# Hybrid decoder trunk on one core: five unread matmuls after the index products, and a separate gate table for the first two expert pairs

## The chip, the core and the metric

The kernel runs on one core of a Trainium2 chip, as one launch that holds the whole network. The metric is the time of one execution in microseconds (us); lower is better. The kernel before takes 1132.8 us in the median of three runs (1131.58 to 1132.91 us).

## What is computed

One decoder layer over 512 tokens of width 1024 in float32: a mixer of two branches, cross-attention into 256 memory tokens, and a mixture of 32 experts. The change lies where the mixture begins:

```python
g_idx = argmax(g_logits); p_g = softmax(g_logits)[g_idx]        # one of 4 groups
e_in_group = take_along_axis(e_logits, g_idx)                   # 8 experts in it
top_v, top_i = lax.top_k(e_in_group, 2)
gate = p_g * softmax(top_v)                                     # two gates per token
# every expert's tokens, in blocks:
xb = xt[tok]; hb = silu(xb @ w1[e]) * (xb @ w3[e]); out = hb @ w2[e]
y[token] += gate * out
```

`xt` is the RMS-normed stream. The kernel gathers rows of the stream that are not normed yet and lets the norm factor of a token (`rr`) travel with its gates.

## The kernel before, in words

The whole program is written out in Python in the order in which each engine is to work; each engine runs its own instructions in that order. TensorE is `PE`, VectorE `DV` (DVE in the profile), ScalarE `AC`, GpSimd `PO` (POOL). Weights arrive by DMAs that SyncE (SP) issues.

**The experts.** An expert's token block holds up to 64 rows (`CAP`); two blocks make a pair and share one gather. For a block, `up` (line 1245) multiplies the gathered rows by w1 and w3: 16 products of 64x512 in full float32, each of which shows as two matmul records, so 32 records; the first 16 use the first halves of w1 and w3, the other 16 the second halves. Then come `act` (silu and product, lines 1256 and 1257), `turn_h` (transposes, lines 1264 and 1267) and `down` (w2, line 1275).

**The weights.** An expert has six tiles of 1 MB (`half_load`, line 733). They go into 19 buffers of that size (`NSLOT`). By the end of the attention part 19 tiles have been asked for; the next two loads are asked for behind the first half of the first `up` (`moe_load(2)` at `k % 4 == 3`), since they need the buffers that this half reads, and so on: every later load waits for a buffer that some product has finished with. SP issues them in order.

**The start of the mixture**, which the change touches:

- The last routing logits are made (line 957), and DVE picks the group and the two experts per token. Meanwhile `warm(..., 4)` (lines 97 to 103) gives TensorE four products of 128x512 whose result nobody reads (`wu`).
- `pp` (line 1037) counts, by 14 small products, the place of each token in its expert's block; `posm` (line 1043) holds the places.
- `tbl` is a table with, for every token, its number (two columns, written early by GpSimd at line 921), the high and low part of its norm factor `rr` (lines 1057 and 1058), and the high and low parts of its gates.
- For the first two pairs, `onehots` (line 1189) makes a matrix that marks which token sits in which place, and `from_tokens` (line 1196) multiplies it with the two number columns of `tbl`: that is the index product. DVE turns its result into an index (line 1201), and GpSimd issues the gather (line 1203).
- `gating` computes the gates (DVE, lines 1063 to 1083) and writes those of the first four experts into `tbl` by `gate_parts` (lines 1054 and 1055).
- `gather_turn` transposes the gathered rows (PE, line 1229) and scales them into `xg` (DVE, line 1185), and `up_of(0)` multiplies them: the first `up`.
- The two gate products (line 1196 again, now 8 columns of `tbl`), `places` (the rest of the routing, DVE, lines 1090 to 1142), and `gates_of` (lines 1215 and 1216), which feeds `act` of the first block, follow.

Of the kernel before, what the change touches and what calls it, by code (L numbers as in the profile page):

```python
# [25 lines left out]
F32 = mybir.dt.float32  # L26
F32R = mybir.dt.float32r
# [3 lines left out]
OP = mybir.AluOpType  # L31
AX = mybir.AxisListType

P = 128
D = 1024
S = 512
T = S // P
# [12 lines left out]
NBLK = NE + 2  # L50
DYN = 4
# [3 lines left out]
def trunk(ctx: ExitStack, tc: tile.TileContext, a: dict, out: bass.AP, dbg=None):  # L55
    nc = tc.nc
    PE, DV, AC, PO = nc.tensor, nc.vector, nc.scalar, nc.gpsimd

    cst = ctx.enter_context(tc.tile_pool(name="cst", bufs=1))
# [25 lines left out]
    def k2(shape, dt=F32, name="k2"):  # L85
        return view(big, shape, dt, name, "k2", 7, (S + 3) * (2 if dt == BF else 1))

    def sm(shape, dt=F32, name="sm"):
        return view(big, shape, dt, name, "sm", 22, 16)

    def md(shape, dt=F32, name="md"):
        return view(big, shape, dt, name, "md", 5, T * NBLK * (2 if dt == BF else 1))

    def bank(shape, dt=F32, name="ps"):
        return view(psp, shape, dt, name, "ps", 8, 512)

    def warm(a_, b_, n, ps=None):

        if ps is None:
            ps = bank([P, 512], name="wu")  # L100
        for _ in range(n):
            PE.matmul(ps, a_, b_, start=True, stop=True)
# [6 lines left out]
    x_sb = cst.tile([P, T, D], F32, name="x_sb")  # L109
# [17 lines left out]
    ident = cst.tile([P, P], F32, name="ident")  # L127
# [784 lines left out]
    rr = cst.tile([P, T], F32, name="rr")  # L912
# [3 lines left out]
    tbl = cst.tile([P, T, 1 + NB, 4], F32R, name="tbl")  # L916
    tk0 = md([P, T, 2], name="tk0")
# [2 lines left out]
            allow_small_or_imprecise_dtypes=True)  # L920
    PO.tensor_copy(tbl[:, :, 0, 0:2], tk0)

    def cols(t, p):
        return tbl[:, t, 0:2 + p:1 + p]

# [73 lines left out]
    def b2(ap, shape):  # L999
        return ap.to_broadcast(shape)  # L1000
# [23 lines left out]
    def spread(dst, src):  # L1024
        DV.tensor_tensor(dst.rearrange("p t (g e) -> p t g e", g=4),
                         goh[:, :, :, None].to_broadcast([P, T, 4, 8]),
                         src[:, :, None, :].to_broadcast([P, T, 4, 8]), op=OP.mult)
# [18 lines left out]
    perm = cst.tile([P, NBLK], F32, name="perm")  # L1046
    permi = cst.tile([P, NBLK], I32, name="permi")

    def gate_parts(b0, b1, src):

        for t in range(T):
            hi, lo = (tbl[:, t, 1 + b0 // 2:1 + b1 // 2, q:4:2] for q in range(2))
            g_ = src[:, t].rearrange("p (n e) -> p n e", e=2)
            DV.tensor_copy(hi, g_)
            DV.tensor_tensor(lo, g_, hi.bitcast(F32), op=OP.subtract)

    DV.tensor_copy(tbl[:, :, 0, 2], rr)
    DV.tensor_tensor(tbl[:, :, 0, 3], rr, tbl[:, :, 0, 2].bitcast(F32), op=OP.subtract)

    def gating():  # L1060

        ge = md([P, T, 4], name="gexp")
        DV.tensor_tensor(ge, gl, b2(gm, [P, T, 4]), op=OP.subtract)
        AC.activation(ge, ge, AF.Exp)
        gs = sm([P, T, 1], name="gsum")
        DV.tensor_reduce(gs, ge, axis=AX.X, op=OP.add)
        dd = sm([P, T, 1], name="dd")
        DV.tensor_sub(dd, m2, m1)
        AC.activation(dd, dd, AF.Exp)
        den = sm([P, T, 1], name="den")  # L1070
        DV.scalar_tensor_tensor(den, dd, 1.0, gs, op0=OP.add, op1=OP.mult)
        g1 = sm([P, T, 1], name="g1")
        DV.reciprocal(g1, den)
        g2 = sm([P, T, 1], name="g2")
        DV.tensor_mul(g2, g1, dd)
        gt8 = md([P, T, 8], name="gt8")
        DV.tensor_tensor(gt8, oh1, b2(g1, [P, T, 8]), op=OP.mult)
        gt8b = md([P, T, 8], name="gt8b")
        DV.tensor_tensor(gt8b, oh2, b2(g2, [P, T, 8]), op=OP.mult)
        DV.tensor_add(gt8, gt8, gt8b)  # L1080
        gate = md([P, T, NE], name="gate")
        spread(gate, gt8)
        DV.tensor_tensor(gate, gate, b2(rr[:, :, None], [P, T, NE]), op=OP.mult)
        gate_parts(0, DYN, gate[:, :, 0:DYN])
        return gate

    def places(gate):

        cnt = md([P, NE], name="cntf")
        DV.tensor_copy(cnt, pp[:, T])  # L1090
        ov = md([P, NE], name="ov")
        DV.scalar_tensor_tensor(ov, cnt, float(CAP), wgt, op0=OP.is_gt, op1=OP.mult)
        DV.tensor_tensor(ov, ov, isp, op=OP.max)
        om = sm([P, 1], name="om")
        DV.tensor_reduce(om, ov, axis=AX.X, op=OP.max)
        DV.tensor_scalar(ov, ov, om, None, op0=OP.is_equal)
        nv = md([P, NE], name="nv")
        DV.tensor_scalar(nv, ov, -1.0, 1.0, op0=OP.mult, op1=OP.add)
        R = 2 * T + 2
        yy = k2([P, R, NE], name="yy")  # L1100
        DV.tensor_tensor(yy[:, 0:T], pp[:, 0:T], off_, op=OP.add)
        DV.tensor_copy(yy[:, T:2 * T], gate)
        DV.tensor_copy(yy[:, 2 * T], cnt)
        DV.tensor_copy(yy[:, 2 * T + 1], io32)
        zz = k2([P, R, NE], name="zz")
        yv = sm([P, R, 1], name="yv")
        DV.tensor_tensor(zz, yy, b2(ov[:, None, :], [P, R, NE]), op=OP.mult)
        DV.tensor_reduce(yv, zz, axis=AX.X, op=OP.add)
        DV.tensor_tensor(zz, b2(yy[:, :, POS:POS + 1], [P, R, NE]), b2(ov[:, None, :], [P, R, NE]), op=OP.mult)
        DV.tensor_tensor(yy, yy, b2(nv[:, None, :], [P, R, NE]), op=OP.mult)  # L1110
        DV.tensor_tensor(yy, yy, zz, op=OP.add)
        DV.tensor_copy(yy[:, :, POS:POS + 1], yv)

        def spaced(dst, src, second, c0=0):

            DV.tensor_copy(dst[:, :, c0:POS + 1], src[:, :, c0:POS + 1])
            DV.tensor_copy(dst[:, :, POS + 2:NBLK - 1], src[:, :, POS + 1:NE])
            DV.tensor_scalar(dst[:, :, POS + 1:POS + 2], src[:, :, POS:POS + 1], second, None, op0=OP.add)

        cn = md([P, 2, NBLK], name="cn")  # L1120
        DV.memset(cn, 0.0)
        spaced(cn[:, 1:2], yy[:, 2 * T + 1:2 * T + 2], 0.0)
        DV.tensor_copy(perm, cn[:, 1])
        DV.tensor_copy(permi, cn[:, 1])
        spaced(posm, yy[:, 0:T], -float(CAP), DYN)
        DV.memset(posm[:, :, NBLK - 1:NBLK], -4096.0)
        gb = md([P, T, NBLK], name="gb")
        DV.memset(gb[:, :, NBLK - 1:NBLK], 0.0)
        spaced(gb, yy[:, T:2 * T], 0.0)
        gate_parts(DYN, NBLK, gb[:, :, DYN:NBLK])  # L1130
        spaced(cn[:, 0:1], yy[:, 2 * T:2 * T + 1], -float(CAP))
        c_ = cn[:, 0]
        DV.memset(c_[:, POS:POS + 1], 0.0)
        nx = k2([P, NBLK, 7], name="nx")
        DV.tensor_tensor(nx, c_[:, :, None].to_broadcast([P, NBLK, 7]),
                         io7[:, None, :].to_broadcast([P, NBLK, 7]), op=OP.is_gt)
        nxr = md([P, NBLK], name="nxr")
        DV.tensor_reduce(nxr, nx, axis=AX.X, op=OP.add)
        one = md([P, NBLK], name="one")
        DV.memset(one, 1.0)  # L1140
        DV.tensor_tensor_scan(cume, one, nxr, 0.0, op0=OP.mult, op1=OP.add)
        DV.tensor_copy(total, cume[:, NBLK - 1:NBLK])
# [44 lines left out]
    def onehots(p):  # L1187
        oh = k2([P, T, 2, CAP], F32R, name="oh")
        DV.tensor_tensor(oh, io64[:, None, None, :].to_broadcast([P, T, 2, CAP]),
                         posm[:, :, 2 * p:2 * p + 2, None].to_broadcast([P, T, 2, CAP]), op=OP.is_equal)  # L1190
        return oh

    def from_tokens(pg, oh, rhs, start=True):

        for t in range(T):
            PE.matmul(pg, oh[:, t].rearrange("p n c -> p (n c)"), rhs(t), start=t == 0, stop=t == T - 1)
# [9 lines left out]
    def tokens_of(pg):  # L1206
        tk = sm([P, 1], name="tk")
        DV.tensor_scalar(tk, pg[:, 0:1], float(S), None, op0=OP.add)
        return tk
# [149 lines left out]
    pgs, gcs, tks, xrs, xgs, ohs, ups = {}, {}, {}, {}, {}, {}, {}  # L1359
# [13 lines left out]
    for p in range(2):  # L1373
        oh = ohs[p] = onehots(p)
        pgs[p] = bank([P, 8], name="pgate")
        from_tokens(pgs[p][:, 0:2], oh, lambda t: tbl[:, t, 0, 0:2])
        xrs[p] = gather_two(pgs[p])
        tks[p] = tokens_of(pgs[p])
    gate = gating()
    xgs[0] = gather_turn(xrs.pop(0))  # L1380
    up_of(0)
    for p in range(2):
        pgs[p] = bank([P, 8], name="pgate")
        from_tokens(pgs[p], ohs.pop(p), lambda t: cols(t, p))
    places(gate)
    for p in range(2):
        gcs[p] = gates_of(pgs[p])
# [5 lines left out]
    for b in range(LASTB + 1):  # L1393
        p, par = divmod(b, 2)
# [23 lines left out]
        if b == LASTB - 2:  # L1418
            left()
            g_f = slot([P, D], name="g_f")  # L1420
            src = a["norm_f_g"]
# [77 lines left out]
```

## Time and profile before

| | |
|---|---|
| median of 3 runs | 1132.8 us (1131.58 to 1132.91) |
| the profiled execution's own time | 1134.74 us |
| its span, first to last instruction | 1132.9 us |
| PE busy | 1092.2 us (96%) |
| DVE busy | 571.9 us (50%) |
| ACT busy | 370.4 us (33%) |
| POOL busy | 117.3 us (10%) |
| granted TensorE clock, mean over the span | 0.988 of full |
| read from HBM | 272.88 MB |

The profile shows one execution. The span is counted from its first instruction to its last; the execution's own time, taken around it, is 1.84 us longer, and it is 1.94 us above the median of the three runs. PE counts as busy while a matmul record is open, so a busy PE need not work at its peak: it also stands so at half clock. The page's slices give the granted clock (PEclk), which here is full nearly throughout and dips around the start of the mixture, and the share of the DMA engines that was busy.

### The profile page before, as it was taken

What the parts mean: (1) busy time and instruction counts of PE and PEld (TensorE: products, weight loads), DVE (VectorE), ACT (ScalarE), POOL (GpSimd) and SP (SyncE); (2) the same over time, 40 slices, a digit from 0 to 9 for tenths busy, and PEclk for the clock granted to TensorE, in tenths of its full rate; (3) what the DMA queues carried; (4) which work ended last, traced back from release to release, by engine and by line L of the source; (5) the groups of instructions that cost most, each with busy time, mean ns of one, the idle gap of its engine ahead of it and who ended that gap; (6) DMA issues with size and microseconds to landing.
All of it is one profiled execution on the core that took longest, in us unless ns stands there. A gap on an engine that the chain in (4) does not pass through costs nothing. (4 is left out here: it accounts for less than half of the span.)

```text
span 1132.9 us, 14115 instructions
## 1 busy us (share of the span) xinstructions
PE 1092.2 (96%) x5297; PEld 725.5 (64%) x5297; DVE 571.9 (50%) x1116; ACT 370.4 (33%) x634; POOL 117.3 (10%) x157
## 2 busy tenths in 40 slices
PE   5999999999999999999999899999999999999995
PEld 4778888888888888898888634444444444443432
DVE  5376574655434566673563464444444444443444
ACT  4366644554442533553443111111111111111112
POOL 4021000200120200000200100000010000000001
PEclk9999999999999999999999889999999999999998
DMA  9122141214323163233249669999999999999981
GB/s 323 51 75 75 53 159 60 75 47 149 112 82 113 38 246 119 88 138 126 81 155 384 240 276 424 426 426 425 426 426 426 425 427 426 425 426 427 426 349 74
DMA packets 62501, 273.29 MB, mean 241 GB/s; under 512 B 6976, under 2 KB 7104, under 8 KB 37856
## 3 DMA queue, kind: packets, MB, share of 16 engines
q1 hardware_dynamic: 57616, 260.15, 57.3%
q0 software_dynamic: 4096, 9.61, 2.4%
q10 hardware_dynamic: 720, 2.62, 0.6%
q8 instruction: 42, 0.69, 0.2%
q14 instruction: 27, 0.22, 0.1%
HBM read 272.88 MB, written 4.19 MB: 245 GB/s over the span
## 5 line engine op out<-in xcount | busy, mean ns | idle before, releaser
L1245 PE MATMUL h<-we,xg 128*64 128x512 f32 x1056 | 240.2, 597 | 6.7 <-DMA we<-in_w 6.1
L1245 PEld LDWEIGHTS h<-we,xg 128*64 128x64 f32 x1056 | 78.4, 138 | 162.0 <-issue 142.5
L276 PE MATMUL acc<-whi,xh 128*128 128x512 f32 x448 | 177.5, 396 | 0.0
L278 PE MATMUL acc<-wlo,xh 128*128 128x512 f32 x448 | 175.3, 391 | 0.7 <-POOL v L379 0.7
L277 PE MATMUL acc<-whi,xl 128*128 128x512 f32 x448 | 175.3, 391 | 0.0
L168 DVE TENSOR_TENSOR wlo<-raw,whi 128x1024 fp32r<-128x1024 f32 x101 | 119.9, 1232 | 47.8 <-ACT whi L167 43.7
L1275 PE MATMUL po<-we,hT 128*64 128x512 f32 x528 | 120.6, 599 | 1.7 <-ACT hT L1267 1.7
L167 ACT CAST whi<-raw 128x1024 fp32r<-128x1024 f32 x104 | 102.9, 1048 | 8.5 <-PE acc L278 4.9
L1282 ACT CAST o_h<-po 64x512 fp32r<-64x512 f32 x66 | 38.2, 579 | 187.9 <-PE po L1275 187.1
L278 PEld LDWEIGHTS acc<-wlo,xh 128*128 128x128 f32 x448 | 84.3, 188 | 19.2 <-POOL v L379 1.1
L277 PEld LDWEIGHTS acc<-whi,xl 128*128 128x128 f32 x448 | 84.5, 189 | 16.5 <-DVE xl L254 0.4
L276 PEld LDWEIGHTS acc<-whi,xh 128*128 128x128 f32 x448 | 84.5, 189 | 16.2 <-ACT xh L253 0.2
L1283 DVE TENSOR_TENSOR o_l<-po,o_h 64x512 fp32r<-64x512 f32 x66 | 45.4, 688 | 74.3 <-ACT o_h L1282 73.2
L1275 PEld LDWEIGHTS po<-we,hT 128*64 128x64 f32 x528 | 35.0, 136 | 65.0 <-issue 53.7
L317 PE MATMUL acc<-xh,whi 128*128 128x512 f32 x192 | 75.3, 392 | 0.4 <-ACT whi L167 0.4
L319 PE MATMUL acc<-xh,wlo 128*128 128x512 f32 x192 | 74.9, 390 | 0.8 <-DVE wlo L168 0.8
L318 PE MATMUL acc<-xl,whi 128*128 128x512 f32 x192 | 74.8, 390 | 0.0
L1267 ACT COPY hT<-phT 128x256 f32<-128x256 f32 x33 | 12.3, 372 | 187.0 <-PE phT L1264 186.9
L1293 DVE TENSOR_TENSOR x_sb<-x_sb,pc 128x512 f32<-128x512 f32 x120 | 72.9, 679 | 0.0
L1185 DVE TENSOR_TENSOR xg<-pgT,g_moe 128x512 f32<-128x512 f32 x34 | 21.9, 686 | 96.6 <-PE pgT L1229 96.6
L1291 PE MATMUL pc<-o_h,ohT 128*128 128x512 f32 x120 | 48.4, 404 | 0.0
L1292 PE MATMUL pc<-o_l,ohT 128*128 128x512 f32 x120 | 47.3, 395 | 0.0
(340 smaller groups left out, 1492.1 us busy)
## 6 DMA issues: line engine op xcount, KB each, us to landing
we<-in_w SPq DMA_DIRECT2D x192, 1024.0 KB, 20.1
raw<-in_w_in SPq DMA_DIRECT2D x31, 1024.0 KB, 5.0
raw<-in_w_xkv SPq DMA_DIRECT2D x8, 1024.0 KB, 4.9
raw<-in_w_out SPq DMA_DIRECT2D x4, 1024.0 KB, 6.4
raw<-in_w_xq SPq DMA_DIRECT2D x4, 1024.0 KB, 6.2
raw<-in_w_xo SPq DMA_DIRECT2D x4, 1024.0 KB, 5.3
x_sb<-in_x SPq DMA_DIRECT2D x4, 512.0 KB, 5.6
xn_d<-x_sb ACTq DMA_DIRECT2D x4, 512.0 KB, 2.9
```

The lines of the kernel that those rows point to most:

```text
L167: AC.copy(hi[:, s], raw[:, s])
L168: (PO if i + q == 1 or (i, q) == (4, 1) else DV).tensor_tensor(lo[:, s], raw[:, s], hi[:, s].bitcast(F32), op=OP.subtract)
L276: PE.matmul(ps, lh, rh, start=first, stop=False)
L277: PE.matmul(ps, ll, rh, start=False, stop=False)
L278: PE.matmul(ps, lh, rl, start=False, stop=last)
L317: PE.matmul(ps[m], hi[:, k, ms], xh, start=first, stop=False)
L318: PE.matmul(ps[m], hi[:, k, ms], xl, start=False, stop=False)
L319: PE.matmul(ps[m], lo[:, k, ms], xh, start=False, stop=last)
L1245: PE.matmul(ps[i * 64:(i + 1) * 64], xg[:, k, xs_], w[n, k // 4][:, k % 4], start=k == 0, stop=k == 7)
L1275: PE.matmul(po[dh][dh * 64:(dh + 1) * 64], hT[:, f], w["2", f // 2][:, f % 2, dh * 512:(dh + 1) * 512], start=f == 0, stop=f == 3)
L1291: PE.matmul(ps, oT_[r, t], o_h[dh][r], start=True, stop=False)
L1293: DV.tensor_add(x_sb[:, t, cs], x_sb[:, t, cs], ps)
```

## The change

There is a second, small table `tb0`, which holds for every token the two number columns, the norm factor's two parts and the gates of the first four experts. GpSimd fills its number columns early, beside those of `tbl`. The index products and the gate products of the first two pairs read `tb0` in place of `tbl`. The two DVE instructions that write the norm factor's parts move from ahead of the index products into `gating`, and write `tb0`. Once `places` has written the gates of the other experts into `tbl`, two DVE copies bring `tb0`'s norm factor and gates over to `tbl`, which the later pairs read as before. And behind the second index product TensorE gets five more unread products of 128x512.

```diff
+    tb0 = cst.tile([P, T, 3, 4], F32R, name="tb0")
+    PO.tensor_copy(tb0[:, :, 0, 0:2], tk0)
...
-    def gate_parts(b0, b1, src):
+    def gate_parts(b0, b1, src, tbl):
...
-    DV.tensor_copy(tbl[:, :, 0, 2], rr)
-    DV.tensor_tensor(tbl[:, :, 0, 3], rr, tbl[:, :, 0, 2].bitcast(F32), op=OP.subtract)
...
         spread(gate, gt8)
+        DV.tensor_copy(tb0[:, :, 0, 2], rr)
+        DV.tensor_tensor(tb0[:, :, 0, 3], rr, tb0[:, :, 0, 2].bitcast(F32), op=OP.subtract)
         DV.tensor_tensor(gate, gate, b2(rr[:, :, None], [P, T, NE]), op=OP.mult)
-        gate_parts(0, DYN, gate[:, :, 0:DYN])
+        gate_parts(0, DYN, gate[:, :, 0:DYN], tb0)
...
-        gate_parts(DYN, NBLK, gb[:, :, DYN:NBLK])
+        gate_parts(DYN, NBLK, gb[:, :, DYN:NBLK], tbl)
+        DV.tensor_copy(tbl[:, :, 0, 2:4], tb0[:, :, 0, 2:4])
+        DV.tensor_copy(tbl[:, :, 1:3], tb0[:, :, 1:3])
...
-        from_tokens(pgs[p][:, 0:2], oh, lambda t: tbl[:, t, 0, 0:2])
+        from_tokens(pgs[p][:, 0:2], oh, lambda t: tb0[:, t, 0, 0:2])
         xrs[p] = gather_two(pgs[p])
         tks[p] = tokens_of(pgs[p])
+    warm(ident, x_sb[:, 0, 0:512], 5)
     gate = gating()
     xgs[0] = gather_turn(xrs.pop(0))
     up_of(0)
     for p in range(2):
         pgs[p] = bank([P, 8], name="pgate")
-        from_tokens(pgs[p], ohs.pop(p), lambda t: cols(t, p))
+        from_tokens(pgs[p], ohs.pop(p), lambda t: tb0[:, t, 0:2 + p:1 + p])
```

How this stands in the engines' own order. On PE, from the index products to the first `up` (`pgate` is their result, `xr` the gathered rows, `pgT` their transposes, `h_...` the result of the first `up`), before:

```order
L1196 MATMUL pgate<-tbl,oh 128x2 x8
L1229 MATMUL pgT<-ident,xr 128x128 x8
L1245 MATMUL h_5247<-we_4783,xg 64x512
L1245 MATMUL h_5247<-we_4785,xg 64x512
...
```

and with the change (`tb_4847` is the tile `tb0`):

```order
L1200 MATMUL pgate<-tb_4847,oh 128x2 x8
L102 MATMUL wu<-x_sb,ident 128x512 x5
L1233 MATMUL pgT<-ident,xr 128x128 x8
L1249 MATMUL h_5255<-we_4783,xg 64x512
L1249 MATMUL h_5255<-we_4785,xg 64x512
...
```

The five products stand between the last index product and the first transpose of gathered rows; nothing else on PE has moved.

On DVE, from the places to the first index, before:

```order
L1043 TENSOR_TENSOR posm<-pp,offm 128x4x4
L1057 CAST tbl<-rr 128x4
L1058 TENSOR_TENSOR tbl<-rr,tbl 128x4
L1189 TENSOR_TENSOR oh<-io_4821,posm 128x512
L1201 TENSOR_SCALAR idx<-pgate 128x1
```

and with the change, there and at the end of `gating`:

```order
L1046 TENSOR_TENSOR posm<-pp,offm 128x4x4
L1193 TENSOR_TENSOR oh<-io_4821,posm 128x512
L1205 TENSOR_SCALAR idx<-pgate 128x1
...
L1028 TENSOR_TENSOR gate<-fm,gt_5224 128x128
L1083 CAST tb_4847<-rr 128x4
L1084 TENSOR_TENSOR tb_4847<-rr,tb_4847 128x4
L1085 TENSOR_TENSOR gate<-gate,rr 128x128
```

The two instructions on `rr` have left the way to the index and stand in front of the product that puts the norm factor on the gates; the two copies into `tbl` (lines 1133 and 1134 of the changed kernel) stand in `places` behind the last gate of `gate_parts`.

## Rows read from the trace of the kernel before

**Rows 1.** Who waited for whom from 660 us to the end: the waits of PE and of its weight loads for expert weights; total us, times, longest.

```profile
PEld h L1245 <- DMA we<-in_w: 13.8, 13, 2.8
PE h L1245 <- DMA we<-in_w: 6.1, 4, 1.9
```

**Rows 2.** Busy time of each engine in long stretches; the last three columns are the granted clock, the busy share of the DMA engines, and GB/s.

```profile
649.00:661.50 12.50, 9.11 (x34) 4.46 (x36) 9.93 (x52) 1.70 (x3) 3.13 (x3) 0.60 0.13 35
663.00:990.00 327.00, 327.00 (x1599) 141.02 (x1596) 147.56 (x335) 53.75 (x97) 23.33 (x24) 1.00 1.01 426
990.00:1090.00 100.00, 93.92 (x435) 40.06 (x433) 39.59 (x86) 13.64 (x25) 6.42 (x7) 1.00 1.01 426
```

**Rows 3.** SyncE's loads of expert weights (line 733) from 640 to 662 us: how many, duration of the issue in ns, first and last start.

```profile
L733 SPq DMA_DIRECT2D we<-in_w x2: 328/356/383, 660.8 to 661.2; - x2
```

**Rows 4.** PE's timeline near the end of the experts: the products of `up` that waited for weights (start, duration, what, in brackets the wait).

```profile
1022.71 3.65 PE L1245 MATMUL h<-we,xg 128*64 128x512 f32 x14 [1.87 <-DMA we<-in_w]
1053.09 3.65 PE L1245 MATMUL h<-we,xg 128*64 128x512 f32 x14 [1.43 <-DMA we<-in_w]
1082.87 3.65 PE L1245 MATMUL h<-we,xg 128*64 128x512 f32 x14 [1.39 <-DMA we<-in_w]
```

**Rows 5.** PE's timeline from the four unread products to the first gathered rows' transposes.

```profile
640.25 6.18 PE L102 MATMUL wu<-x_sb,ident 128*128 128x512 f32 x8
646.27 0.51 PE L1037 MATMUL pp<-A,tri 128*128 128x32 bf16 x14
648.01 0.58 PE L1196 MATMUL pgate<-tbl,oh 128*128 128x2 f32 x4 [1.23 <-DVE oh L1189]
649.60 0.98 PE L1196 MATMUL pgate<-tbl,oh 128*128 128x2 f32 x4 [1.01 <-DVE oh L1189]
653.11 1.97 PE L1229 MATMUL pgT<-ident,xr 128*128 128x128 f32 x8 [2.52 <-DMA xr<-xn_d,idx]
```

**Rows 6.** Half-microsecond stretches, same columns as rows 2: the granted clock (third from the right) where it changes.

```profile
645.00:645.50 0.50, 0.50 (x2) 0.09 (x1) 0.00 (x0) 0.00 (x0) 0.00 (x0) 0.70 0.97 410
648.50:649.00 0.50, 0.09 (x1) 0.00 (x1) 0.38 (x3) 0.00 (x0) 0.00 (x0) 0.71 0.82 344
650.50:651.00 0.50, 0.08 (x1) 0.00 (x0) 0.31 (x3) 0.00 (x0) 0.49 (x2) 0.50 0.00 0
658.50:659.00 0.50, 0.50 (x4) 0.18 (x2) 0.47 (x2) 0.00 (x0) 0.00 (x0) 0.55 0.00 0
```

**Rows 7.** PE's weight loads of the last of the four unread products, at the lower clock and then at the higher (one load per record, two per product; the last row is the load of what comes next).

```profile
643.81 0.34 PEld L102 LDWEIGHTS wu<-x_sb,ident 128*128 128x128 f32 x1 [0.52 <-issue]
644.66 0.34 PEld L102 LDWEIGHTS wu<-x_sb,ident 128*128 128x128 f32 x1 [0.52 <-issue]
645.41 0.19 PEld L102 LDWEIGHTS wu<-x_sb,ident 128*128 128x128 f32 x1 [0.41 <-issue]
645.84 0.10 PEld L1037 LDWEIGHTS <-tri 128*128 128x128 bf16 x1 [0.24 <-issue]
```

**Rows 8.** PE's weight loads of the first `up` and of the second: the first four loads, and the 17th and 18th, which open the second half.

```profile
655.34 0.30 PEld L1245 LDWEIGHTS h<-we,xg 128*64 128x64 f32 x4 [0.67 <-DVE xg L1185]
660.17 0.14 PEld L1245 LDWEIGHTS h<-we,xg 128*64 128x64 f32 x2 [0.29 <-issue]
665.12 0.20 PEld L1245 LDWEIGHTS h<-we,xg 128*64 128x64 f32 x4
668.17 0.14 PEld L1245 LDWEIGHTS h<-we,xg 128*64 128x64 f32 x2 [0.28 <-DMA we<-in_w]
```

**Rows 9.** DVE from the places to the first one-hot matrix, and at the end of `gating`.

```profile
646.81 0.17 DVE L1043 TENSOR_TENSOR posm<-pp,offm 128x16 f32<-128x16 f32 x1 [2.16 <-PE pp L1037]
646.90 0.16 DVE L1057 CAST tbl<-rr 128x4 fp32r<-128x4 f32 x1
647.10 0.17 DVE L1058 TENSOR_TENSOR tbl<-rr,tbl 128x4 fp32r<-128x4 f32 x1
647.18 0.68 DVE L1189 TENSOR_TENSOR oh<-io,posm 128x512 fp32r<-128x512 f32 x1
654.60 1.29 DVE L1185 TENSOR_TENSOR xg<-pgT,g_moe 128x512 f32<-128x512 f32 x2
```

**Rows 10.** The same transposes and scaling for the second pair, at full clock: PE and DVE.

```profile
672.52 1.16 PE L1229 MATMUL pgT<-ident,xr 128*128 128x128 f32 x8
673.27 1.29 DVE L1185 TENSOR_TENSOR xg<-pgT,g_moe 128x512 f32<-128x512 f32 x2 [6.25 <-PE pgT L1229]
```

**Rows 11.** PE's first matmuls of the whole program, one row each (products of 128x512 in fp32r; start to start is 0.43 us at the lower clock and 0.23 us at the higher).

```profile
11.59 0.79 PE L276 MATMUL acc<-whi,xh 128*128 128x512 f32 x1
13.33 0.63 PE L276 MATMUL acc<-whi,xh 128*128 128x512 f32 x1
13.76 0.44 PE L277 MATMUL acc<-whi,xl 128*128 128x512 f32 x1
14.03 0.40 PE L278 MATMUL acc<-wlo,xh 128*128 128x512 f32 x1
```

**Rows 12.** What follows `places` on DVE (the first gates of `gates_of`, the second half of `act`), and PE's first transposes that need `act`.

```profile
664.78 0.15 DVE L1215 TENSOR_REDUCE gc<-pgate 64x1 f32<-64x2 f32 x1
666.27 0.76 DVE L1257 SCALAR_TENSOR_TENSOR hh<-h,gc,hh 64x512 f32<-64x512 f32 x1
672.13 0.46 PE L1264 MATMUL phT<-ident,hh 64*128 64x64 f32 x4
```

## The prediction

> **What bounds the kernel now.** I read the waits of the second half of the program first. From 660 us on nearly the only waits of PE for something other than itself are for expert weights: 6.1 us by its matmuls, and some by its weight loads beside them [rows 1]. They lie late: at 1022.71, 1053.09 and 1082.87 the second half of an `up` waits 1.4 to 1.9 us for its tile [rows 4]. The reader is to see that these starts are about 30 us apart, two experts' time, which is the rhythm of the transfers and not of PE. The long stretches say the same: from 663 to 1090 us the DMA engines are full (share 1.01, 426 GB/s), and in the last 100 us of that PE is busy 93.92 of 100 us [rows 2]. So the end is set by a stream of weights that never pauses once it runs. Then I asked when it starts to run. From 649 to 661.5 us it stands still (share 0.13, 35 GB/s) [rows 2], and its next load is issued at 660.8 [rows 3]: all buffers are full, and the first comes free when the first half of the first `up` is through. The 17th weight load of that `up`, which opens its second half, stands at 660.17 [rows 8], 0.6 us ahead of the issue. **That point, 660.17, is what the change has to move.** PE has 6.1 us of waits to give, so a later start of PE by less does no harm by itself, and an earlier one no good; but an earlier or later first half moves the whole stream, and with it the end, one for one.
>
> The stage ahead of it comes from PE's timeline: unread products to 646.4, small counting products, the two index products (done at 650.58), then 2.52 us of waiting for the gather, the transposes at 653.11 and the first `up` at 655.34 [rows 5, 8]. The granted clock falls from 1.00 to 0.50 at about 648.7 and is back only at about 658.95 [rows 6], so the wait itself, the transposes and over half of the first half run at 1.2 GHz.
>
> **The index, earlier.** The two DVE instructions on `rr` leave the way to the one-hot matrix. They occupy 646.90 to 647.27, but overlap with their neighbours: the matrix starts at 647.18, and without them it can start when `posm` is done (646.98) plus the 0.04 us that a dependent instruction takes there (647.06 to 647.10), so at 647.02 [rows 9]. That is 0.16 us; the bounds are 0 and 0.28 (its start in the place of the first of them). I take 0.16, since the matrix needs `posm`. Index products, index and gather follow by the same amount: the last index product ends at 650.42, the gather is there at 652.95.
>
> **The five products.** They start at 650.42 and must be through before the transposes, whatever the gather does, since PE works in order. The wait that they fill lasts 2.5 us. Their own time depends on the clock, which is 0.50 when they start [rows 6]. At that level a record takes 0.85 us (643.81 to 644.66) and a product, two records, 1.71; at full clock a record takes 0.43 (645.41 to 645.84) and a product 0.86 [rows 7]. If the clock rises d us after the first of them, d/1.71 of them are done by then and the rest take 0.86 each: together 4.3 + d/2. So even at full clock from the start they outlast the wait by 1.8 us; the question is whether the clock that they win pays for it.
>
> Three rises in this trace bound d. After the program's first product (11.59) the spacing halves behind 13.76: 2.2 us [rows 11]. After the first product of the first `up` (655.34) it takes 3.6 us, after the four unread products began (640.25) 5.05 us (to 645.3) [rows 5, 6, 8]. So the five products take 5.4, 6.1 or 6.8 us and end at 655.8, 656.5 or 657.2. I take 3.6: it is the middle one, and its place is the same one in the program, after the same wait; the two others are the ends.
>
> The Trainium skill (TensorE: Matmul & The Clock Gate, Part 4) says that transposes do not count as a busy PE for the clock the way matmuls do. The trace neither confirms nor contradicts it: the clock rose 5.85 us after the first transpose of gathered rows and 3.6 us after the first product. If transposes counted, that rise would be one of d = 5.85, and the sum by it would come to +2.0 us in place of +0.9.
>
> **Transposes and scaling.** They now run at full clock. There DVE's scaling starts 0.75 us after the first transpose (672.52 to 673.27) [rows 10], and `up` starts 0.74 us after the scaling (654.60 to 655.34) [rows 8, 9]: 1.5 us from the last unread product to the first `up`, against 2.2 before. In the old timeline part of the 2.2 was DVE finishing `gating`; that, with the two moved instructions (at most 0.33 us), is now done near 654.8, ahead of the scaling, and costs nothing. If the products were so fast that this cover went, it would cost 0.1 to 0.3 us.
>
> **The first half of the first `up`.** At full clock its second half opens 3.05 us after its start (665.12 to 668.17 in the second `up`); before it took 4.83 (655.34 to 660.17) [rows 8]. That is the gain: 1.78 us.
>
> **The sum.** 650.42 + 6.1 + 1.5 + 3.05 = 661.07, against 660.17: **0.9 us later**. With d = 2.2 it is +0.2, with 5.05 it is +1.6. The weight stream starts so much later, and the end moves with it. The profiled span of 1132.9 us becomes 1133.8, its own time of 1134.74 becomes 1135.6; the median shown is 1.94 us below that own time, so the forecast is 1132.8 + 0.9 = **1133.7 us**.
>
> **The rest of the change at nothing.** The copy that GpSimd makes into `tb0` lies in the setup of an engine that is busy a tenth of the time. The gate products read a table of other name and the same width. The two copies in `places` put DVE back by some 0.3 us, and `places` itself starts 2.7 us later behind the later scaling. Queued behind it are `gates_of` and `act` of the first block; `act` ended at 667.03 and PE wants it at 672.13 [rows 12], so about 3 us of cover are left, counting that PE too is later. Beyond those 3 us it would cost one for one. No DMA is added or reordered; the gathers and the loads keep their places in the queues of POOL and SP.
>
> **Rivals.** *The clock rises early.* If it comes at once or within 2 us, the five products take 4.3 to 5.3 us and the sum is -0.9 to +0.1. For it: the index products just ahead are also work, and d was 2.2 at the start of the program. Against it: the two rises in this stage took 3.6 and 5.05. The Trainium skill (the same page, Part 1) says that the number of matmuls run before the rise varies between runs of one kernel; the trace agrees, with its three delays.
>
> *Slower than before: the clock falls again behind the five products.* Between the last of them and the first `up` lie 1.5 us of transposes and of waiting for DVE. The fall at 648.7 came 2.3 us after the four unread products ended, with small products and 1.2 us of waiting between [rows 5, 6]. If that happens here, the first half runs slowly once more, 4.83 us or longer in place of 3.05, and the sum is +2.7 us or more: 1135.5. The point from which it decides is the granted clock between the end of the products and the 17th load of `up`. Against it: at 1022.71 PE had waited 1.87 us [rows 4] in a stretch where the clock stayed at 1.00 [rows 2].
>
> *Nothing reaches the end.* If the stream's start were not what sets the end (if it could be made up in 430 us), the time would stay at 1132.8. The DMA engines' share of 1.01 throughout leaves nothing to make it up with.
>
> **How the numbers follow.** A difference of about 0.2% (2.27 us) is what a measurement of this kernel can tell from no change. Chances: the forecast, d from 2.2 to 5.05, +0.2 to +1.6 us: 0.60. Early rise, -0.9 to +0.1: 0.24. The clock falls again, +2.7 or more: 0.10. Nothing reaches the end: 0.06. The runs of before lie 1.33 us apart, so I give each case some 0.7 us of scatter. Faster by over 0.2% would need the early rise and more than that scatter: 0.05. Slower by over 0.2% holds most of the falling clock and a little of the forecast's upper end: 0.11. The rest, 0.84, is within 0.2%. The range reaches from 1132.8 - 0.9 - 0.7 = 1131.2 to the falling clock's 1135.5; what it leaves out is a longer fall and scatter at both ends.
>
> **What would show it.** Right: five products that outlast the gather by some 3 us, and reach full clock on the way; the whole first `up` in about 6.9 us; its second half opening 10.0 to 11.4 us behind the end of the index products (before 9.6, 650.58 to 660.17); the first late load and the end later by as much; PE's late waits for weights still there. Wrong: the first half opening earlier than that; a clock of 0.50 in the first `up`; the late waits gone; or an end that moves by another amount than the weight stream's start.

## The result, and the profile after

The changed kernel takes 1140.26 us in the median of 5 runs (1139.83 to 1145.0); the kernel before 1132.76 us (1131.58 to 1132.91). The ratio is 1.0075, with a 95% interval of 1.0062 to 1.0089: 7.5 us slower by the medians and 7.0 to 10.1 us by the interval, where 0.9 us was forecast and 1135.5 us was the upper end of the range. The profiled execution has a span of 1137.1 us and a time of its own of 1139.83 us.

The stage that the change was aimed at is over sooner in this execution than in the profile before. PE's timeline, from the four unread products on (start, duration, what, in brackets the wait), and the weight load that opens the second half of the first `up`:

```profile
639.21 5.38 PE L102 MATMUL wu<-x_sb,ident 128*128 128x512 f32 x8
647.59 0.58 PE L1200 MATMUL pgate<-tb,oh 128*128 128x2 f32 x4 [1.01 <-DVE oh L1193]
648.03 4.54 PE L102 MATMUL wu<-x_sb,ident 128*128 128x512 f32 x10
652.41 1.05 PE L1233 MATMUL pgT<-ident,xr 128*128 128x128 f32 x8
653.79 7.09 PE L1249 MATMUL h<-we,xg 128*64 128x512 f32 x32 [0.34 <-DVE xg L1189]
656.85 0.14 PEld L1249 LDWEIGHTS h<-we,xg 128*64 128x64 f32 x2 [0.29 <-DVE zz L1109]
```

The five products take 4.54 us, which is full clock throughout, and the first `up` takes 7.09 us in place of 8.86. The index products, too, end at 648.17 and not at 650.58 [rows 5]: here the four unread products ahead of them ran partly at full clock (5.38 us against 6.18). The granted clock in the stretches of [rows 6], third from the right:

```profile
645.00:645.50 0.50, 0.00 (x0) 0.00 (x0) 0.47 (x2) 0.00 (x0) 0.00 (x0) 1.00 1.09 459
648.50:649.00 0.50, 0.50 (x3) 0.21 (x2) 0.16 (x3) 0.22 (x1) 0.49 (x2) 1.00 0.63 262
650.50:651.00 0.50, 0.50 (x2) 0.19 (x1) 0.50 (x2) 0.14 (x1) 0.50 (x1) 1.00 0.14 41
```

So the stream of weights starts earlier, by 3.3 us: 2.4 us of them lie ahead of the new products (the earlier end of the index products), 0.9 us behind. The row that answers to [rows 3], SyncE's loads:

```profile
L733 SPq DMA_DIRECT2D we<-in_w x4: 328/355/383, 657.5 to 661.3; - x4
```

And yet the span is 4.2 us longer and the execution's own time 5.1 us. (The medians lie 7.5 us apart, since the execution profiled before is 1.94 us above its median and this one 0.43 us below.) The long stretches that answer to [rows 2] show where (last three columns: granted clock, DMA share, GB/s):

```profile
663.00:990.00 327.00, 324.96 (x1574) 139.18 (x1572) 145.08 (x326) 53.47 (x97) 23.34 (x24) 0.99 1.01 420
990.00:1090.00 100.00, 93.65 (x427) 38.20 (x424) 38.26 (x83) 13.62 (x26) 6.41 (x7) 1.00 1.01 420
```

The DMA engines are as full as before (share 1.01), but they move 420 GB/s and not 426. Over the 427 us from 663 to 1090, 426/420 makes 6.1 us. PE's waits for weights, which answer to [rows 1], have grown with it, from 6.1 to 8.3 us:

```profile
PEld h L1249 <- DMA we<-in_w: 18.5, 16, 2.9
PE h L1249 <- DMA we<-in_w: 8.3, 7, 2.0
```

And PE is out of weights far sooner: before it is busy all of the stretch up to 990 us [rows 2], now its busy time falls near 852 us (same columns as above):

```profile
849.00:852.00 3.00, 3.00 (x15) 1.32 (x11) 1.46 (x3) 0.68 (x1) 0.00 (x0) 1.00 1.01 411
852.00:853.50 1.50, 0.49 (x2) 0.00 (x0) 0.00 (x0) 0.00 (x0) 0.00 (x0) 1.00 1.03 426
```

The early start is not what does this: in the profiles below that move 426 GB/s, PE's first wait of over 0.5 us for weights ends at 987.6 to 992.1 us, however early the stream starts; in the four that move 420 it ends at 854.5 to 858.1.

Nothing in the diff touches a transfer. What it does touch is the layout of SBUF, the memory on the chip that the weights are loaded into. `tb0` is 3 x 4 x 4 float32 per partition, 192 bytes, in the pool of constants (`cst`), and all that is allocated behind it moves by so much. The pool behind it (`big`) holds the 19 weight buffers, and in the compiled program they have moved: the first from byte 57344 of a partition to 57536, the others likewise. 57344 is 7 x 8192, and a buffer is 8192 bytes, so all 19 had lain at multiples of 8192, and now none lies at a multiple of 256. The kernel even holds a constant tile of 63 columns of which 7 are used (`io7`, line 897): its unused tail sets this place.

### The profile page after: what moved, and what is told of

It is laid out like the page before. It is cut to its first block, busy times and chain, and to the rows that moved or that the text cites. A ratio compares the mean times of both kernels' runs of the same rounds, so it can differ in the third digit from the quotient of the medians.

```text
span 1137.1 us, 14139 instructions
## 1 busy us (share of the span) xinstructions
PE 1097.0 (96%) x5307; PEld 725.4 (64%) x5307; DVE 572.2 (50%) x1118; ACT 370.5 (33%) x634; POOL 118.5 (10%) x158
## 5 line engine op out<-in xcount | busy, mean ns | idle before, releaser
L1249 PE MATMUL h<-we,xg 128*64 128x512 f32 x1056 | 243.2, 597 | 9.1 <-DMA we<-in_w 8.3
```

The source lines that it names most:

```text
L1249: PE.matmul(ps[i * 64:(i + 1) * 64], xg[:, k, xs_], w[n, k // 4][:, k % 4], start=k == 0, stop=k == 7)
```

## The experiments

Theory A: the place of the weight buffers sets the rate of the stream, and the change moved them. Rival B: the new start of the mixture (products, table, copies) delays the stream in a way that the profiled execution hides. Rival C: the rate differs between executions or chips, whatever the kernel. The runs below are each compared with runs of the kernel before on the same chip.

**The changed kernel with its buffers put back.**

```diff
-    io7 = cst.tile([P, 63], F32, name="io7")[:, 0:7]
+    io7 = cst.tile([P, 15], F32, name="io7")[:, 0:7]
```

> The changed kernel with 192 bytes per partition taken out of an unused tail of another constant tile (io7, 63 columns to 15), so that the 19 weight buffers lie again at multiples of 8192 bytes as before the change. Theory A (place): the weight stream was slowed from 426 to 420 GB/s because the new table moved the buffers by 192 bytes; here it runs at 426 GB/s from 663 to 990 us, and the time falls by 6 to 7 us to 1131.5 to 1134 us. Rival B (start): the unread products or the table's copies delay the stream; the rate stays what it was in the changed kernel and so does the time, about 1140 us. Rival C (the rate differs from execution to execution or chip to chip, whatever the kernel): rate and time fall anywhere between.

Measured: 1133.62 us against 1132.64 us, ratio 1.0010 (1.0001 to 1.0018). The rate is back:

```profile
663.00:990.00 327.00, 325.70 (x1590) 140.26 (x1587) 145.44 (x322) 53.28 (x97) 23.33 (x24) 1.00 1.01 426
990.00:1090.00 100.00, 95.17 (x442) 41.14 (x440) 43.82 (x95) 13.64 (x25) 6.42 (x7) 1.00 1.01 425
```

The whole change without the shift costs 0.1%, and rival B falls with it.

**The kernel before with its buffers moved.**

```diff
-    io7 = cst.tile([P, 63], F32, name="io7")[:, 0:7]
+    io7 = cst.tile([P, 111], F32, name="io7")[:, 0:7]
```

> The kernel before with nothing changed but 48 more unused columns in io7: its weight buffers lie 192 bytes further on, where the change put them. Theory A: 420 GB/s in place of 426 from 663 to 990 us, and about 6 us more: 1138 to 1140 us, as the changed kernel without its products. Rivals B and C: 426 GB/s and 1132.8 us.

Measured: 1140.95 us, ratio 1.0071 (1.0059 to 1.0083), with no other change than 48 unread columns:

```profile
663.00:990.00 327.00, 325.02 (x1576) 138.38 (x1576) 145.11 (x325) 53.78 (x97) 23.37 (x24) 1.00 1.01 420
990.00:1090.00 100.00, 92.57 (x421) 38.63 (x418) 38.06 (x83) 13.36 (x25) 6.42 (x7) 1.00 1.01 420
```

Taken with the first run this shows the shift as the cause from both sides: 426 to 420 by the shift alone, and back. The time lies 1 us above the 1138 to 1140 us that were expected. The shift moves everything behind `io7`, not the 19 buffers alone; that it acts through them is inferred, since they are what the stream writes, and was not tested apart.

**The five products alone.** In the kernel before, with `warm(ident, x_sb[:, 0, 0:512], 5)` put where the change has it.

```diff
         tks[p] = tokens_of(pgs[p])
+    warm(ident, x_sb[:, 0, 0:512], 5)
     gate = gating()
```

> The kernel before with the five unread products alone (one table, norm factor where it was, buffers where they were). Theory A with the terms of the prediction: 426 GB/s, the first half of the first up through 0.2 to 1.8 us later against the end of the index products if the clock has to rise again, 0.8 us earlier if it does not fall there; 1132 to 1134.5 us. Rival B: 1139 us or more.

Measured: 1133.37 us against 1132.64, ratio 1.0009 (1.0000 to 1.0018), 426 GB/s: between nothing and 2 us.

**The table alone.** The first run's kernel without the five products.

```diff
-    warm(ident, x_sb[:, 0, 0:512], 5)
```

> The changed kernel with the buffers back at multiples of 8192 and without the five products: the second table, the norm factor behind the index and the two copies alone. Theory A: 426 GB/s and 0 to 0.3 us faster than before, 1132.5 to 1132.8 us, no difference that can be measured. Rival B, if it is the copies: 1135 us or more.

Measured: 1133.63 us, ratio 1.0003 (0.9992 to 1.0013), 426 GB/s. That is above the 1132.5 to 1132.8 us that were expected, but the kernel before scatters by more than this difference. In the time, the table, the moved norm factor and the copies make no difference that can be told from nothing. But the median is that of the first run (1133.62), so the 0.1% there can't be put down to the products alone. The profiles do show a small cost of the table, at the very end. PE's last `up`, in a profile without the table and in one with it (the kernels with three products, further down), and the weight load in the middle of the second that waits:

```profile
1091.77 7.09 PE L1245 MATMUL h<-we,xg 128*64 128x512 f32 x32 [0.34 <-PEq L1349]
```

```profile
1091.44 7.81 PE L1249 MATMUL h<-we,xg 128*64 128x512 f32 x32 [0.34 <-PEq L1353]
1095.61 0.29 PEld L1249 LDWEIGHTS h<-we,xg 128*64 128x64 f32 x4 [0.57 <-SPq L1353]
```

The last `up` takes 7.09 us in all seven profiles without the table, 7.81 to 7.84 in the five with the table and the buffers in place, 8.04 in that of the changed kernel. Why the table makes this load wait, no run here shows.

**Which places are good?** The kernel before with `io7` of 79, 95 and 127 columns, so that the buffers lie 64, 128 and 256 bytes beyond multiples of 8192.

```diff
-    io7 = cst.tile([P, 63], F32, name="io7")[:, 0:7]
+    io7 = cst.tile([P, 79], F32, name="io7")[:, 0:7]      # 95, 127 in the two others
```

> The kernel before with 16 more unused columns in io7: weight buffers 64 bytes beyond multiples of 8192. If the stream wants multiples of 128, 256 or more, it runs at 420 GB/s as with 192 bytes and the time is 1138 to 1141 us; if 192 is bad for another reason than its remainder by 128 (say by a collision that depends on the distance), 426 GB/s and 1132.6 us are possible.

> The same with 32 more columns: 128 bytes beyond multiples of 8192. If multiples of 128 are enough: 426 GB/s and 1132.6 us. If it takes 256 or more: 420 GB/s or between, and 1136 to 1141 us.

> The same with 64 more columns: 256 bytes beyond multiples of 8192. If multiples of 128 or 256 are enough: 426 GB/s and 1132.6 us. If it takes 512 or more: 420 GB/s or between, 1136 to 1141 us.

Measured: with 64 bytes 1140.39 us, ratio 1.0064 (1.0049 to 1.0080); with 128 bytes 1138.11 us, 1.0051 (1.0035 to 1.0066); with 256 bytes 1132.45 us, 1.0004 (0.9994 to 1.0013). The first stretch of each, in this order:

```profile
663.00:990.00 327.00, 325.12 (x1583) 139.00 (x1580) 145.27 (x330) 51.92 (x94) 23.35 (x24) 1.00 1.01 420
```

```profile
663.00:990.00 327.00, 324.97 (x1576) 138.31 (x1573) 145.49 (x322) 53.43 (x97) 23.34 (x24) 1.00 1.01 420
```

```profile
663.00:990.00 327.00, 325.95 (x1590) 139.65 (x1588) 145.45 (x322) 53.34 (x97) 23.33 (x24) 1.00 1.01 426
```

A remainder of 64, 128 or 192 by 256 gives 420 GB/s; a remainder of 0 gives 426, and a multiple of 8192 isn't needed. The times of the three bad places differ by up to 2.8 us, with 4 to 6 runs each and not all on one chip; their rates, and the rests in the table below, hardly do.

**Three products in place of five**, in the first run's kernel and in the kernel before:

```diff
-    warm(ident, x_sb[:, 0, 0:512], 5)
+    warm(ident, x_sb[:, 0, 0:512], 3)
```

This is the edit in the first run's kernel; in the kernel before, the line with 3 is new.

> The changed kernel with the weight buffers back at multiples of 8192 and three unread products in place of five. At full clock they take 2.6 us, about the wait for the gather (2.5 to 3.1 us), so nothing hangs over; if the clock then stays up, the first up starts no later than without them and runs at full clock: 1130.5 to 1132.5 us, faster than both kernels by 0.5 to 2 us. If the clock is down when they start, they take up to 5.1 us and the clock may not rise before the first up: 1133 to 1135 us.

> The kernel before with three unread products behind the index products and nothing else. If the gain of the run with three products comes from the products: 1131.5 to 1132.5 us, 0.999 of before. If it comes from the norm factor behind the index (at most 0.3 us by the rows) or is scatter: 1132.6 us or more.

Measured: 1131.79 us against 1132.95, ratio 0.9990 (0.9980 to 1.0000); and without the table 1131.16 against 1132.29, ratio 0.9992 (0.9983 to 1.0001). Each leans to 1 us faster at the edge of what can be told; the second lies 0.3 us below what was expected. That both lean the same way, with and without the table, speaks for the products; the table's part is too small to show in these times. In the profile of the first the clock fell behind the start of the three products, they took 4.14 us, and the first `up` still ran at full clock (7.09 us). PE's timeline of the second, where the clock stayed up:

```profile
648.25 2.82 PE L102 MATMUL wu<-x_sb,ident 128*128 128x512 f32 x6
651.44 1.13 PE L1229 MATMUL pgT<-ident,xr 128*128 128x128 f32 x8 [0.37 <-DMA xr<-xn_d,idx]
```

There three products fill the wait to within 0.37 us and hang over nothing.

**Two more profiles of the five products** (the first run's kernel once more, unchanged, so there is no diff).

> A second look at the changed kernel with its buffers back at multiples of 8192, for an execution whose clock falls at another place. If the products' overhang is what costs the 1 us that the executions show on average, an execution whose granted clock is 0.50 when the five products start takes 5.4 to 6.8 us for them, and its span is 1131 us or more; one whose clock stays up repeats 4.5 us and 1129.5 us.

> A third look at the same kernel, with the same expectations as the second.

Measured: 1133.4 and 1133.71 us, spans 1131.4 and 1131.7. In both the clock fell just behind the start of the products. The first of them, PE's timeline, the weight load that opens the second half of the first `up`, and the granted clock:

```profile
646.62 0.58 PE L1200 MATMUL pgate<-tb,oh 128*128 128x2 f32 x4 [1.01 <-DVE oh L1193]
647.05 6.24 PE L102 MATMUL wu<-x_sb,ident 128*128 128x512 f32 x10
653.13 1.04 PE L1233 MATMUL pgT<-ident,xr 128*128 128x128 f32 x8
```

```profile
657.57 0.14 PEld L1249 LDWEIGHTS h<-we,xg 128*64 128x64 f32 x2 [0.29 <-DVE zz L1109]
```

```profile
648.50:649.00 0.50, 0.50 (x2) 0.34 (x1) 0.43 (x5) 0.50 (x1) 0.27 (x1) 0.50 0.92 172
652.00:652.50 0.50, 0.50 (x3) 0.22 (x2) 0.00 (x0) 0.00 (x0) 0.00 (x0) 1.00 0.01 0
```

6.24 us for the products, and 10.4 us from the end of the index products (647.20) to the second half (657.57).

**All profiles in one table.** Start: the first load behind the first half of the first `up`. Rest: the span's end less the start.

| run | buffers modulo 256 | start, us | rest, us | GB/s, 663 to 990 |
|---|---|---|---|---|
| before | 0 | 660.8 | 472.1 | 426 |
| after | 192 | 657.5 | 479.6 | 420 |
| changed, buffers back | 0 | 656.5 | 473.0 | 426 |
| the same, second profile | 0 | 658.2 | 473.2 | 426 |
| the same, third profile | 0 | 658.3 | 473.4 | 426 |
| before, +192 bytes | 192 | 658.5 | 479.0 | 420 |
| before, five products | 0 | 657.8 | 472.4 | 426 |
| table, no products | 0 | 661.1 | 473.2 | 426 |
| before, +64 bytes | 64 | 660.8 | 478.8 | 420 |
| before, +128 bytes | 128 | 657.0 | 479.1 | 420 |
| before, +256 bytes | 0 | 657.5 | 472.4 | 426 |
| table, three products | 0 | 656.4 | 473.1 | 426 |
| before, three products | 0 | 656.8 | 472.3 | 426 |

The rest falls into four groups. With the buffers at a remainder of 0 it is 472.1 to 472.4 us without the table and 473.0 to 473.4 with it; with the buffers shifted, 478.8 to 479.1 without and 479.6 with. So the shift costs between 6 and 7 us wherever it stands, and the table some 0.8 us, of which the last `up` above is 0.7. This also speaks against rival C: over all thirteen profiles the rate goes by the place of the buffers alone.

## Why the prediction was wrong

**What bounds the kernel: right.** The end is the start of the weight stream plus a rest that stays the same while rate and table do. The rest column shows it over a spread of nearly 5 us in the start, and a rate 1.4% lower goes to the end almost undiminished.

**The step that failed: "The rest of the change at nothing."** It priced the new table by its instructions (a GpSimd copy, a name, two DVE copies; in the time, the run with the table alone can't be told from nothing) and said of the stream that no DMA is added or reordered. It took from that, without a sentence for it, that the stream keeps its rate. A tile of 192 bytes has a second effect, on the address of all that is allocated behind it, and through 19 buffers on every weight transfer. That is +6.9 us in the rest (472.1 to 479.0 by the shift alone). The issues of the 173 late loads take 6.6 us of it, from the first one's start to the last one's end, in the kernel before and with the shift alone:

```profile
660.79 422.48 SPq L733 DMA_DIRECT2D we<-in_w  x173
```

```profile
658.52 429.12 SPq L733 DMA_DIRECT2D we<-in_w  x173
```

The last 0.3 us are not traced to a place. Under the same heading falls the 0.8 us of the table in the rest: it was put at nothing, and why it is there stays open. No rival held the shift: the third came as far as the sentence that full DMA engines leave nothing to make a delay up with, and did not ask what a slower full stream would cost.

The Trainium skill (DMA: Bandwidth & Descriptors, How a descriptor splits into AXI transactions) has a rule that bears on this: a transfer is cut into pieces of 256 bytes that begin at multiples of 256, and where one doesn't start on such a multiple, bytes ahead of its start are fetched for nothing and cost time. It says so of what a transfer reads; what moved here is the place that it writes. The boundary agrees with the runs (0 and 256 good; 64, 128 and 192 not). As an estimate from its beat counts, 8192 bytes would take 258, 260 or 262 beats (of 32 bytes) in place of 256 at 64, 128 and 192, so 0.8, 1.6 and 2.3% more; the runs show one and the same 1.4% (426 to 420) for all three, and the measurement decides. Had the addresses been read with it, theory A would have stood among the rivals.

**The five products: the mechanism right, the size not settled.** With the buffers in place they cost 1.0009 (1.0000 to 1.0018) alone, which holds the +0.9 us that was forecast and nearly nothing too; the first run, which has them, and the run with the table alone have the same median. The two profiles with a falling clock show the mechanism as it was priced: 6.24 us (5.4 to 6.8 given, 6.1 taken), 1.2 us and not 1.5 from the products to the first `up` (653.29 to 654.51), and 10.4 us to the second half (10.0 to 11.4 given). The profiled execution of the changed kernel is the rival in which the clock rises early, at its very end: the clock didn't fall behind the index products, and the second half opens at 656.85, 8.7 us behind the index products, 0.9 us less than before. So executions of both kinds go into the measured time, and that it lies near +0.9 is in part luck. The rival of a clock that falls again between the products and the first `up` showed in none of the five profiles with five products. The sentence that the delays vary between executions rested on three delays of one trace, which can't show that; the profiles of the last section do.

**The index earlier by 0.16 us:** the one-hot matrix did start 0.04 us behind the end of `posm` (645.17 against 645.13 in the trace of the changed kernel), as worked out, and the first index product starts 1.6 us behind the start of the counting products (644.42 to 646.01) where it was 1.74 (646.27 to 648.01). On the time it can't be told from nothing.

## What to carry to other kernels

A tile's size is also an address. Before an allocation is called free, print where everything behind it comes to lie, and try the buffers that a saturated stream of transfers writes at multiples of 256 bytes: in this kernel 0 and 256 bytes beyond a multiple were good, 64, 128 and 192 were not, and 192 bytes in a table cost 6.9 us where all the rest of the change came to about 1 us. And where the end is a stream's start plus a rest, a change can be read in two numbers, start and rest, before any question of mechanism.

## What the runs showed of the hardware that I had not expected

- The start of the stream moved between 657.0 and 660.8 us among five profiles of the same instructions (before, and before with 64, 128, 192 and 256 more bytes), by where the granted clock fell and rose around the unread products. The prediction's rows came from one of the two with the latest start: the four unread products took 6.18 us there, and 5.38 us in the run with 192 bytes. A single profile of this stage is good to no better than some 4 us.
- The five products took 4.54 us in one profile and 6.24 us in another of the very same kernel, with the clock falling just behind their start in the second. What decides between the two the runs don't show.
- The slow stream kept the DMA engines' busy share at the same 1.01. The share tells that the engines are full, not that they are fast; only the GB/s beside it showed the loss. Packet by packet the trace shows it too: one of 8192 bytes took 309.6 ns in the mean before and 314.3 ns with the shift alone (663 to 990 us).
